# Opening products of two projection pairs moved into the end of the scan stage, and the block sums of the input loaded whole on GpSimd's queue

## The chip, the cores and the metric

The kernel runs on one core of one Trainium2 chip. The metric is the device time of one execution in microseconds (us), the median over several runs; lower is better. The engines of the core are PE (TensorE, matrix products), DVE (VectorE), ACT (ScalarE), POOL (GpSimd) and SP (SyncE, which here only issues DMAs). Each takes its own instructions in order. A DMA can be issued from several engines' queues; this kernel issues nearly all from SP, and eight accumulating stores from POOL.

## The reference

One layer of an encoder on 1024 tokens and 16 learned meta tokens, in float32, with a model width of 1024:

```python
h = rmsnorm(h_res, norm1_w[l])
proj = h @ w_in[l]
(q, k, v, z, b_raw, a_raw, sc_b, sc_c, sc_x, gate_a, gate_b) = jnp.split(proj, SPLIT_POINTS, axis=-1)
o_dn = gated_deltanet_bidir(q, k, v, z, b_raw, a_raw, ...)
y_a = o_dn @ w_branch_dn[l]
y_b = (sc_b * depthwise_conv_centred(sc_c * sc_x, sc_conv_w[l])) @ w_branch_sc[l]
merged = jax.nn.sigmoid(gate_a) * y_a + jax.nn.sigmoid(gate_b) * y_b
h_res = h_res + merged @ w_out[l]
gu = rmsnorm(h_res, norm2_w[l]) @ w_gate_up[l]
h_res = h_res + (jax.nn.silu(gu[..., :D_FF]) * gu[..., D_FF:]) @ w_down[l]
```

The gated DeltaNet has eight heads with a forward and a backward scan over chunks of 64 tokens; its output is normalized per head and multiplied by silu(z). A final norm follows, and the meta tokens are dropped.

## The kernel before, in words

**Stage 1** runs the eight heads' scans. Between the small products of the scans PE works through a stream of dense projections (L345): units of 128 columns of `w_in`, first those that the heads need (q, k, v), then `fill_units` (the short convolution, some gates, and z of the first `ZH` heads). Each unit's weights, 128x1024, are loaded by `pick` on SP into one of a few rotating `raw` slots and split in quarters into a high and a low part by `split_part`: ACT casts half of the chunk (128x512), DVE subtracts, twice. Every float32 product is made of three matmuls (high by high, high by low, low by high). A planner with a time per engine decides during the build what comes next; the instructions then stand in a fixed order on each engine.

A head ends with `outputs()`, its norm (`norm()` in `g_scan`: L942, L945, a root on small tiles at L516 to L521, then eight scalings at L950), eight transposes on PE (L98) into two banks, two copies `vS` (L965) and two stores of o_d. z of the same heads is finished by L481 (ACT), L485 and L487 (DVE) and stored in z_d.

The block sums of the input's four quarters (for the scheme below) are made early in stage 1 and stored in DRAM, as four tiles `tx_d0` to `tx_d3`.

**The border and stage 2.** The remaining projections are made in pairs: two units `rg` and `ru` of `w_in` by all 1024 tokens, as a 2x2 block product with seven block products instead of eight. P1 and P2 are plain blocks of rg by blocks of the input; S1 to S4 take sums of weight blocks (S4 by a plain input block), TT takes the plain last block of ru; T1 to T4 are the input's sums. Each of them is twelve matmuls of 128x512 (`product`, L1552). The first two pairs are z of the last heads ("z pairs", n = 0 and 1), then come the gates (n = 2, 3, ...). The engines' order at the border is written out by hand in `SECTION`, one name a step, the pair's number behind it: `h`, `l` split rg whole (ACT L1599, DVE L179, 128x1024); `uh`, `ul` split ru's last block (128x512, L1608); `b1` to `b4` are the weight sums on DVE (128x512 each, in place in rg and ru); `sah`, `sal`, `sbh`, `sbl` split those sums (L1616, 128x1024 each); `T1h` and `T1l`, and so on, split the input's sums (ACT L1573, DVE L179, 128x2048 each); `P1`, `P2`, `S1` to `S4`, `TT` are the products on PE; `c` and `a` take results out of the banks (L1629 on ACT, L1518 on DVE); the rest finishes outputs.

The tiles that these steps share are eight large homes (`b0` to `b3`, `mA`, `mB` and others): a step that writes a home waits until its last reader is through. In the kernel before, the sums are loaded at the border by 16 DMAs of 256 KB on SP (L1576), behind the last head's stores and ahead of the second pair's weights (L1593). The first pair's weights are loaded, and rg of them split, in stage 1.

Of the kernel before, what the change touches and what calls it, by code (L numbers as in the profile page):

```python
# [8 lines left out]
F32 = mybir.dt.float32  # L9
# [7 lines left out]
P = 128  # L17
D = 1024
# [30 lines left out]
def encoder_layer(ctx: ExitStack, tc: tile.TileContext, x, meta, norm1_w, w_in, w_ba,  # L49
# [442 lines left out]

    def cs(c):
# [302 lines left out]
    def g_scan(h, st_):  # L796
# [162 lines left out]
        for c4 in range(2):  # L959
            oT = vS[:, 4 * c4:4 * c4 + 4]  # L960
            pt = newbank()
            for c in range(4):
                transpose(pt[:, c], oacc[4 * c4 + c])
            yield pe(430)
            nc.scalar.copy(oT, pt)  # L965
            A(512)
            nc.sync.dma_start(o_d[h][:, c4 * 512:(c4 + 1) * 512].rearrange("p (c t) -> p c t", c=4), oT)
# [22 lines left out]
    def pick():  # L990
# [46 lines left out]
    def g_input_sums():  # L1037
# [17 lines left out]
        for k in range(4):  # L1055
            for x in range(2):
# [7 lines left out]
                for i in range(2):  # L1064
                    nc.sync.dma_start(part_of(tx_d[k][:, i], x), r[:, i])
                yield T["pe"] + LAND
# [489 lines left out]
    def moving_steps():  # L1556
# [3 lines left out]
        for i in range(2):  # L1560
            for j in range(2):
                mov[f"B{i + 1}{j + 1}"] = hx[0][:, 4 * i:4 * i + 4, c[j]], [hx[1][4 * i + k][:, c[j]] for k in range(4)]
        for g, n in (("b0", "T1"), ("b1", "T2"), ("mA", "T3")):
            t = big(g, [P, 2, 4, 512])
            mov[n] = t[:, 0], t[:, 1]
        x, y = (big(g, [P, 2, 4, 512], F32) for g in ("b2", "b3"))
        raws_ = {"T2": x[:, 0], "T1": x[:, 1], "T3": y[:, 0], "T4": y[:, 1]}

        def high(n, t):
            if n == "T4":  # L1570
                m = big("b2", [P, 2, 4, 512])
                mov[n] = m[:, 0], m[:, 1]
            nc.scalar.copy(mov[n][0], t)  # L1573
        for n, (r, c) in (("T2", (1, right)), ("T1", (0, left)), ("T3", (0, right)), ("T4", (1, left))):
            for k in range(4):
                nc.sync.dma_start(raws_[n][:, k], tx_d[k][:, r, c])  # L1576
# [3 lines left out]
    raw_slots.extend((tp, f"raw{i}") for i in range(2))  # L1580
    left, right = slice(0, 512), slice(512, 1024)
# [6 lines left out]
    def pair_steps(n, j, z=False):  # L1588

        A_, a = {}, {}  # L1590
        rg, ru = (rawtile([P, KT, P]) for _ in range(2))
        for r, off in zip((rg, ru), (OZ, OZ + P) if z else (OGA, OGB)):
            nc.sync.dma_start(r, w_in[unit(off + j * P)])  # L1593
        g0, g1, u0, u1 = rg[:, 0:4], rg[:, 4:8], ru[:, 0:4], ru[:, 4:8]
# [6 lines left out]
        def corner():  # L1601
            if n == 0:
                u = big("w2", [P, 2, 4, P])
                u_hl[0] = u[:, 0], u[:, 1]
            elif n == 1:
                u_hl[1] = [tp.tile([P, 4, P], F32R, tag="t2", name=uid("u_hl"), bufs=2) for _ in range(2)]
            A_["A22"] = u_hl[n % 2]
            nc.scalar.copy(u_hl[n % 2][0], u1)  # L1608
# [9 lines left out]
        def out_tile(k):  # L1618
            if k not in a:
                a[k] = s4()  # L1620
            return a[k]
# [57 lines left out]
    def last_pair(n, j):  # L1679
# [29 lines left out]
    SECTION = """  # L1709
        P1_0 uh_0 ul_0 b1_0 b2_0 P2_0 b3_0 h_1 b4_0 c1_0 l_1 sah_0 P1_1 sbh_0 sal_0 T2h sbl_0 a1_0 P2_1 T2l T1h  # L1710
        S2_0 T1l T3h uh_1 T3l S1_0 c2_0 T4h ul_1 S3_0 b1_1 c3_0 c1_1 b2_1 h_2 a1_1 h1_0 S4_0 l_2 h1_1 T4l P1_2 b3_1
        sbh_1 a3_0 b4_1 h3_0 P2_2 s1_0 sah_1 sbl_1 c1_2 sal_1 TT_0 a2_0 s1_1 h2_0 a1_2 s2_0 S2_1 uh_2 h4_0 ul_2 h1_2
        b1_2 b2_2 S1_1 c2_1 b3_2 sbh_2 b4_2 s3_0 sah_2 S3_1 sbl_2 c3_1 sal_2 S4_1 a3_1 s4_0 h3_1 s3_1 TT_1 a2_1 h2_1
        s2_1 S2_2 h4_1 s4_1 S1_2 c2_2 h_3 S3_2 l_3 c3_2 S4_2 a3_2 h3_2 TT_2 a2_2 h2_2 h4_2
    """
    first = [pair_steps(0, ZH, True)[0]]
    moving_steps()
    first.append(pair_steps(1, ZH + 2, True)[0])
# [56 lines left out]
    def head_load(h):  # L1775

        if not og:
            og.extend(big(f"b{2 + i}", [P, 4, SEQ], F32) for i in range(2))
        if h < ZH:
# [26 lines left out]
    def next_part():  # L1806
# [592 lines left out]
```

## Time and profile before

| | |
|---|---|
| median of 3 runs | 1971.52 us (1971.27 to 1975.44) |
| the profiled execution's own time | 1974.82 us |
| its span | 1972.8 us, mean granted clock 0.992 |
| PE busy | 1939.6 us, 98% of the span |
| DVE, ACT, POOL busy | 1481.7, 880.6, 116.3 us |
| stage 1's last dense matmul (L345) starts | 924.40 us |
| third pair's first product starts | 968.69 us |

The profile comes from the one execution of 1974.82 us. In its timeline a row has the start, the duration, the engine, the line, the operation with output and inputs, the count, and in brackets the engine's idle time ahead with what ended it. In the table of waits a row has the engine and line that waited, what released it, then us in all, how often, and the longest. L12 is line 12 of the kernel before; behind the change the lines are up to some 30 higher.

### The profile page before, as it was taken

Reading aid. Unit: us, or ns where it says so; the run is one execution under the profiler, and the core shown is the slowest. Engines: PE = TensorE matmul, PEld = TensorE weight load, DVE = VectorE, ACT = ScalarE, POOL = GpSimd, SP = SyncE. Lnnn points to the kernel's source line nnn. Section 1 sums busy time; section 2 is a strip of 40 time slices with the busy share of each in tenths; the row PEclk is TensorE's granted clock in tenths of the full one; section 3 lists DMA queues with packets and bytes.
Section 4 is the critical chain, followed back from the end, with each engine's and each line's share of the span. In section 5 each row is a group of like instructions: output and inputs, shape, how many; then the busy total and the mean of one; then the engine's idle time right before and its main releaser. Section 6 shows DMA issues by size and latency. Waiting matters only on the chain.

```text
span 1972.8 us, 32276 instructions
## 1 busy us (share of the span) xinstructions
PE 1939.6 (98%) x11872; PEld 1702.2 (86%) x11872; DVE 1481.7 (75%) x3158; ACT 880.6 (45%) x2026; POOL 116.3 (6%) x418
## 2 busy tenths in 40 slices
PE   9999999999999999999799999999999999999998
PEld 8998999999999999887688878788888888888886
DVE  7888688898989888867666688669676766746575
ACT  6462354636464646343444544235333333325344
POOL 2012201010101010200000000000000000000000
PEclk9999999999999999999899999999999999999999
DMA  4266322223232223376457955233366654577654
GB/s 145 67 173 153 92 87 81 98 81 97 81 108 60 76 60 98 114 260 226 156 190 271 355 205 183 95 100 115 108 232 246 245 182 160 175 280 240 195 175 163
DMA packets 155299, 307.13 MB, mean 156 GB/s; under 512 B 47932, under 2 KB 57589, under 8 KB 151685
## 3 DMA queue, kind: packets, MB, share of 16 engines
q1 hardware_dynamic: 153397, 299.83, 45.2%
q0 software_dynamic: 1152, 4.19, 1.3%
q8 instruction: 93, 1.52, 0.3%
q10 hardware_dynamic: 592, 1.05, 0.1%
q14 instruction: 65, 0.53, 0.1%
HBM read 211.60 MB, written 93.41 MB: 155 GB/s over the span
## 4 chain that ended last, share of the span: by engine, by line
PE 85%; DMA 6%; DVE 6%; issue 1%; ACT 1%; SPq 0%; DVEq 0%; ACTq 0%
PE pm L345 31%; PE pd L1552 13%; PE pe L1552 7%; PE pm L1552 4%; PE pe L612 1%; PE pd L914 1%; PE pd L893 1%; PE pd L875 1%; PE pd L878 1%; PE pe L2306 1%; PE pe L2308 1%; PE pe L2307 1%; PE pd L910 1%; PE pd L98 1%; PE pd L2306 1%
## 5 line engine op out<-in xcount | busy, mean ns | idle before, releaser
L345 PE MATMUL pm<-al,wh 128*128 128x320 f32 (+4 forms) x1248 | 426.5, 347 | 0.0
L345 PE MATMUL pm<-hTh,wh 128*128 128x320 f32 (+4 forms) x1248 | 425.5, 346 | 0.5 <-ACT hTh L1188 0.5
L345 PE MATMUL pm<-hTh,wl 128*128 128x320 f32 (+4 forms) x1248 | 424.3, 345 | 0.0
L345 PEld LDWEIGHTS pm<-hTh,wh 128*128 128x128 f32 x1248 | 233.7, 188 | 11.4 <-ACT hTh L1188 1.3
L345 PEld LDWEIGHTS pm<-hTh,wl 128*128 128x128 f32 x1248 | 233.9, 188 | 10.0
L345 PEld LDWEIGHTS pm<-al,wh 128*128 128x128 f32 x1248 | 233.9, 188 | 9.9
L102 DVE TENSOR_TENSOR al<-raw,ring_h 128x1024 fp32r<-128x1024 f32 x73 | 88.6, 1222 | 65.1 <-ACT ring_h L101 64.5
L101 ACT CAST ring_h<-raw 128x1024 fp32r<-128x1024 f32 x73 | 76.7, 1053 | 107.5 <-PE pd L2308 38.7
L367 DVE SCALAR_TENSOR_TENSOR kq<-ra,wc,kq 128x520 f32<-128x520 f32 x128 | 96.6, 754 | 3.6 <-ACT kq L397 2.1
L900 ACT ACTIVATE w<-pd,small 128x128 f32<-128x128 f32 x128 | 39.9, 363 | 126.7 <-PE pd L893 126.4
L1007 DVE TENSOR_TENSOR wl<-raw,wh 128x512 fp32r<-128x512 f32 x112 | 75.6, 686 | 18.7 <-ACT wh L1010 18.3
L505 DVE TENSOR_TENSOR tm<-fP,fN 128x135 f32<-128x135 f32 (+23 forms) x248 | 72.3, 292 | 7.3 <-DMA fN<-nd 2.0
L509 DVE TENSOR_TENSOR fP<-fP,tm 128x135 f32<-128x135 f32 (+23 forms) x248 | 71.9, 290 | 5.2
L1010 ACT CAST wh<-raw 128x512 fp32r<-128x512 f32 x112 | 66.3, 626 | 3.7 <-issue 3.6
L865 ACT ACTIVATE jk<-NP 128x128 f32<-128x128 f32 x64 | 19.9, 311 | 90.5 <-DVE NP L861 89.4
L2246 ACT ACTIVATE b<-b 128x512 f32<-128x512 f32 x20 | 12.6, 632 | 105.2 <-DVE b L1518 105.2
L1518 DVE TENSOR_TENSOR b<-pd,b 128x512 f32<-128x512 f32 x21 | 14.5, 689 | 51.9 <-PE pd L1552 51.8
L1552 PE MATMUL pd<-b_hl,wh 128*128 128x512 f32 x168 | 51.9, 390 | 0.0
L102 DVE TENSOR_TENSOR al<-raw,parts_h 128x1024 fp32r<-128x1024 f32 x28 | 33.5, 1218 | 24.3 <-ACT parts_h L101 24.3
L367 DVE SCALAR_TENSOR_TENSOR vT<-ra,wc,vT 128x520 f32<-128x520 f32 x64 | 48.3, 755 | 3.4 <-ACT vT L397 2.3
L555 ACT ACTIVATE PQ<-PQ,negG 128x128 f32<-128x128 f32 x128 | 43.3, 395 | 16.8 <-DVE PQ L550 16.7
L701 POOL TENSOR_TENSOR tm<-mP,mN 1x15 f32<-1x15 f32 (+7 forms) x120 | 37.2, 310 | 205.9 <-DMA mN<-ndm 197.6
(678 smaller groups left out, 4853.3 us busy)
## 6 DMA issues: line engine op xcount, KB each, us to landing
raw<-in_w_in_dram SPq DMA_DIRECT2D x72, 512.0 KB
raw<-in_w_gate_up_dram SPq DMA_DIRECT2D x44, 512.0 KB
sums<-in_w_down_dram SPq DMA_DIRECT2D x22, 512.0 KB
t_d<-sums SPq DMA_DIRECT2D x11, 1024.0 KB
raw<-s_d SPq DMA_DIRECT2D x44, 256.0 KB
raw<-t_d SPq DMA_DIRECT2D x44, 256.0 KB
act_d<-b SPq DMA_DIRECT2D x43, 256.0 KB
raw<-act_d SPq DMA_DIRECT2D x33, 256.0 KB
```

The costliest lines, as they stand in the source:

```text
L101: nc.scalar.copy(hi, src)
L102: nc.vector.tensor_tensor(out=lo, in0=src, in1=hi.bitcast(F32), op=ALU.subtract)
L345: mm(po[:, :n], ww[:, k], f(k)[:, t0:t0 + n], start=i == 0, stop=i == 3 * KT - 1)
L367: nc.vector.scalar_tensor_tensor(out=acc, in0=raw[:, h0 + t:h0 + t + hn], scalar=wc[:, t, col:col + 1], in1=acc, op0=ALU.mult, op1=ALU.add)
L505: nc.vector.tensor_tensor(out=tv, in0=fP[:, 0:r, j:j + 1].broadcast_to([P, r, n]), in1=fN[:, j:j + 1, j + 1:32].broadcast_to([P, r, n]), o ...
L509: nc.vector.tensor_tensor(out=fP[:, 0:r, j + 1:32], in0=fP[:, 0:r, j + 1:32], in1=tv, op=ALU.subtract)
L555: nc.scalar.activation(PQ[:, c, d], PQ[:, c, d], AF.Exp, bias=negG2[:, c, hd:hd + 1])
L900: nc.scalar.activation(w[d], b2[:, 2 + d], AF.Copy, scale=ce[:, c, d:d + 1])
L1007: nc.vector.tensor_tensor(out=u[1][1][:, k], in0=u[2][:, k], in1=u[1][0][:, k].bitcast(F32), op=ALU.subtract)
L1010: nc.scalar.copy(u[1][0][:, k], u[2][:, k])
L1552: mm(po, x[:, k], at(y, k), start=i == 0 and not add_to, stop=i == 11, skip_group_check=add_to)
L2306: mm(bank[t], h_[:, c], h_[:, hi], start=first, stop=False)
```

## The change

1. Two more units are appended to the dense stream, `u_open` for rg of both z pairs. They are held until the last head's `outputs()` are through (`tail["on"]`) and then make P1 and P2 of both pairs (48 matmuls). Their weights are loaded by `pick` and split by `split_part` in stage 1.
2. `tx_d` becomes one tile in DRAM; each of the four sums is loaded whole, 1 MB in rows of 2 KB, by one DMA on GpSimd's queue. ru of both z pairs is loaded behind them on the same queue.
3. The last head's transposes go to the two `pe` banks instead of those of its scan.
4. `SECTION` has a new order, and the homes of T1 to T4, of the pair sums and of some later tiles are renamed to fit.

The diff, cut to its core:

```diff
-    tx_d = [dr.tile([P, 2, D], F32, name=f"tx_d{i}") for i in range(4)]
+    tx_d = dr.tile([4, P, 2, D], F32, name="tx_d")
...
+    tail, opened = {"on": False}, []
+
+    def u_open(w):
+
+        while not tail["on"]:
+            T["pe"] += 100
+            yield
+        a = {"g": w, "bank": pss(), "p2": psm()}
+        opened[[x.get("g") for x in opened].index(None)].update(a)
+        c = slice(C0 + META, C0 + META + 512)
+        for po, k0 in ((a["bank"], 0), (a["p2"], 4)):
+            for i in range(12):
+                k, m = k0 + i // 3, i % 3
+                mm(po, w[m == 2][:, k], hx[0][:, k, c] if m != 1 else hx[1][k][:, c], start=i == 0, stop=i == 11)
+                pe(227)
+                yield
...
         outputs()
+        tail["on"] = h == H - 1
...
-            pt = newbank()
+            pt = psd().rearrange("p (a n) -> p a n", a=4) if h == H - 1 else newbank()
...
+    fill_units += [(OZ + h * P, u_open, None, None) for h in (ZH, ZH + 2)]
...
         nc.sync.dma_start(raw, w_in[unit(u[0])])
+        if u[1] is u_open:
+            opened.append({"raw": raw})
...
-        for g, n in (("b0", "T1"), ("b1", "T2"), ("mA", "T3")):
-            t = big(g, [P, 2, 4, 512])
-            mov[n] = t[:, 0], t[:, 1]
-        x, y = (big(g, [P, 2, 4, 512], F32) for g in ("b2", "b3"))
+        t = big("b0", [P, 2, 4, 512])
+        mov["T1"] = t[:, 0], t[:, 1]
+        x, y = (big(g, [P, 2, 4, 512], F32) for g in ("b1", "mA"))
+        t = big("b2", [P, 2, 4, 512])
+        mov["T2"] = t[:, 0], t[:, 1]
...
-        for n, (r, c) in (("T2", (1, right)), ("T1", (0, left)), ("T3", (0, right)), ("T4", (1, left))):
-            for k in range(4):
-                nc.sync.dma_start(raws_[n][:, k], tx_d[k][:, r, c])
+        for n, (r, c) in (("T3", (0, right)), ("T4", (1, left)), ("T2", (1, right)), ("T1", (0, left))):
+            nc.gpsimd.dma_start(raws_[n], tx_d[:, :, r, c].rearrange("k p c -> p k c"))
...
-        rg, ru = (rawtile([P, KT, P]) for _ in range(2))
-        for r, off in zip((rg, ru), (OZ, OZ + P) if z else (OGA, OGB)):
-            nc.sync.dma_start(r, w_in[unit(off + j * P)])
+        if z:
+            rg, ru = opened[n]["raw"], rawtile([P, KT, P])
+            nc.gpsimd.dma_start(ru, w_in[unit(OZ + P + j * P)])
+            a.update({k: opened[n][k] for k in ("g", "bank", "p2")})
...
     SECTION = """
-        P1_0 uh_0 ul_0 b1_0 b2_0 P2_0 b3_0 h_1 b4_0 c1_0 l_1 sah_0 P1_1 sbh_0 sal_0 T2h sbl_0 a1_0 P2_1 T2l T1h
-        S2_0 T1l T3h uh_1 T3l S1_0 c2_0 T4h ul_1 S3_0 b1_1 c3_0 c1_1 b2_1 h_2 a1_1 h1_0 S4_0 l_2 h1_1 T4l P1_2 b3_1
...
+        uh_0 ul_0 b1_0 T2h b2_0 b3_0 b4_0 c1_0 T2l sah_0 sbh_0 sal_0 S2_0 T1h sbl_0 T3h T1l S1_0 c2_0 a1_0 uh_1 T3l
+        T4h h_2 S3_0 c3_0 T4l ul_1 l_2 S4_0 a3_0 b1_1 c1_1 h1_0 b2_1 P1_2 b3_1 sbh_1 b4_1 h3_0 sah_1 a1_1 P2_2 sbl_1 c1_2
...
```

**PE at the end of stage 1.** Before, behind the last dense matmul (NP is the head's output, ident the identity of a transpose; pd, pe and pm are banks):

```order
L345 MATMUL pm_12188<-hTh,wl_11936 128x512
L98 MATMUL pd_12282<-ident,NP_10513 128x128 x4
L98 MATMUL pd_12289<-ident,NP_10513 128x128
L1552 MATMUL pd_12346<-hTh,wh_12342 128x512
L98 MATMUL pd_12289<-ident,NP_10513 128x128 x3
L1552 MATMUL pd_12346<-al_148,wh_12342 128x512
```

With the change, first the start of the 24 matmuls that follow the last dense one, then, of the second pair's, the place of the transposes and the end:

```order
L345 MATMUL pm_12191<-hTh,wl_11933 128x512
L506 MATMUL pd_12273<-hTh,wh_12102 128x512
...
L506 MATMUL pd_12320<-al_145,wh_12271 128x512
L98 MATMUL pe_12334<-ident,NP_10510 128x128 x4
L506 MATMUL pd_12320<-hTh,wl_12272 128x512
L98 MATMUL pe_12342<-ident,NP_10510 128x128 x4
L506 MATMUL pm_12321<-hTh,wh_12271 128x512
...
L506 MATMUL pm_12321<-hTh,wl_12272 128x512
L1573 MATMUL pd_12273<-b_2080_12373,b_2081_12378 128x512 x12
```

The transposes stood ahead of nearly all opening products; now 35 of the 48 stand ahead of them, and the product behind the last (L1573) is S2 of the first pair.

**The loads.** Before, on SP, behind the last stores:

```order
L489 DMA z_d_114<-rb_12265 128x512
L967 DMA o_d_126<-vS_11705 128x512 x2
L1576 DMA b_2072_12312<-tx_d_91 128x512
L1576 DMA b_2072_12312<-tx_d_92 128x512
...
L1593 DMA raw_12330<-in_w_in_dram 128x1024
L1593 DMA raw_12331<-in_w_in_dram 128x1024
```

Now they are the last DMAs on POOL, behind two memsets of the last head:

```order
L745 MEMSET XT_11423 32x8x32
L1597 DMA mA_12372<-tx_d 128x4x512 x2
L1597 DMA b_2078_12371<-tx_d 128x4x512 x2
L1614 DMA raw_12379<-in_w_in_dram 128x1024
L1614 DMA raw_12381<-in_w_in_dram 128x1024
```

Nothing on POOL's queue waits for the last head's stores of o_d any more; ru of the first pair (the first L1614) stands behind all four sums.

**DVE at the border.** With the change, from the last small operation of the root on:

```order
L538 SCALAR_TENSOR_TENSOR small_10219<-small_10219 128x9
L968 TENSOR_SCALAR NP_10510<-NP_10510,small_10219 128x128 x7
L1028 TENSOR_TENSOR wl_12272<-raw_12104,wh_12271 128x512 x2
L968 TENSOR_SCALAR NP_10510<-NP_10510,small_10219 128x128
L179 TENSOR_TENSOR w_2088_12387<-raw_12379,w_2088_12387 128x512
L1539 TENSOR_TENSOR raw_12379<-raw_12379 128x512
L179 TENSOR_TENSOR raw_12379<-raw_11934,raw_12379 128x512
L179 TENSOR_TENSOR raw_11934<-raw_12379,raw_11934 128x512
L179 TENSOR_TENSOR raw_11934<-raw_11934 128x512
L179 TENSOR_TENSOR b_2080_12373<-b_2078_12371,b_2080_12373 128x2048
L179 TENSOR_TENSOR b_2081_12378<-raw_11934,b_2081_12378 128x1024
```

Before, the eight scalings (there L950) stood in one row and the weight sums followed; the low half of the second pair's rg (there one subtraction of 128x1024) came behind the sums. Now its two halves stand ahead of the last scaling, and T2's low part (128x2048) ahead of the pair sum's (the last row). In the orders after the first pairs no instruction has moved on any engine.

More of the change, by code (lines that the diff above doesn't have):

```diff
@@ L1064, in g_input_sums @@
                 for i in range(2):
-                    nc.sync.dma_start(part_of(tx_d[k][:, i], x), r[:, i])
+                    nc.sync.dma_start(part_of(tx_d[k, :, i], x), r[:, i])
                 yield T["pe"] + LAND
@@ L1590, in pair_steps @@
         A_, a = {}, {}
-        rg, ru = (rawtile([P, KT, P]) for _ in range(2))
-        for r, off in zip((rg, ru), (OZ, OZ + P) if z else (OGA, OGB)):
-            nc.sync.dma_start(r, w_in[unit(off + j * P)])
+        if z:
+            rg, ru = opened[n]["raw"], rawtile([P, KT, P])
+            nc.gpsimd.dma_start(ru, w_in[unit(OZ + P + j * P)])
+            a.update({k: opened[n][k] for k in ("g", "bank", "p2")})
+            gh, gl = a["g"]
+            A_["A11"], A_["A12"] = (gh[:, 0:4], gl[:, 0:4]), (gh[:, 4:8], gl[:, 4:8])
+        else:
+            rg, ru = (rawtile([P, KT, P]) for _ in range(2))
+            for r, off in ((rg, OGA), (ru, OGB)):
+                nc.sync.dma_start(r, w_in[unit(off + j * P)])
         g0, g1, u0, u1 = rg[:, 0:4], rg[:, 4:8], ru[:, 0:4], ru[:, 4:8]
@@ L1601, in corner @@
         def corner():
[L1602 to L1606, printed above, removed]
             A_["A22"] = u_hl[n % 2]
@@ L1619, in out_tile @@
             if k not in a:
-                a[k] = s4()
+                a[k] = first_out if n == 0 and k == "o1" else s4()
             return a[k]
@@ L1709, in encoder_layer @@
     SECTION = """
-        P1_0 uh_0 ul_0 b1_0 b2_0 P2_0 b3_0 h_1 b4_0 c1_0 l_1 sah_0 P1_1 sbh_0 sal_0 T2h sbl_0 a1_0 P2_1 T2l T1h
-        S2_0 T1l T3h uh_1 T3l S1_0 c2_0 T4h ul_1 S3_0 b1_1 c3_0 c1_1 b2_1 h_2 a1_1 h1_0 S4_0 l_2 h1_1 T4l P1_2 b3_1
-        sbh_1 a3_0 b4_1 h3_0 P2_2 s1_0 sah_1 sbl_1 c1_2 sal_1 TT_0 a2_0 s1_1 h2_0 a1_2 s2_0 S2_1 uh_2 h4_0 ul_2 h1_2
-        b1_2 b2_2 S1_1 c2_1 b3_2 sbh_2 b4_2 s3_0 sah_2 S3_1 sbl_2 c3_1 sal_2 S4_1 a3_1 s4_0 h3_1 s3_1 TT_1 a2_1 h2_1
+        uh_0 ul_0 b1_0 T2h b2_0 b3_0 b4_0 c1_0 T2l sah_0 sbh_0 sal_0 S2_0 T1h sbl_0 T3h T1l S1_0 c2_0 a1_0 uh_1 T3l
+        T4h h_2 S3_0 c3_0 T4l ul_1 l_2 S4_0 a3_0 b1_1 c1_1 h1_0 b2_1 P1_2 b3_1 sbh_1 b4_1 h3_0 sah_1 a1_1 P2_2 sbl_1 c1_2
+        sal_1 s1_0 TT_0 a2_0 h1_1 h2_0 a1_2 S2_1 s2_0 h4_0 s1_1 uh_2 ul_2 S1_1 c2_1 h1_2 b1_2 b2_2 b3_2 sbh_2 b4_2 s3_0 sah_2
+        S3_1 sbl_2 c3_1 sal_2 S4_1 a3_1 s4_0 h3_1 s3_1 TT_1 a2_1 h2_1
         s2_1 S2_2 h4_1 s4_1 S1_2 c2_2 h_3 S3_2 l_3 c3_2 S4_2 a3_2 h3_2 TT_2 a2_2 h2_2 h4_2
     """
-    first = [pair_steps(0, ZH, True)[0]]
     moving_steps()
-    first.append(pair_steps(1, ZH + 2, True)[0])
+    first_sums = big("b3", [P, 2, 2, KT, P])
+    first = [pair_steps(n, ZH + 2 * n, True)[0] for n in range(2)]
+    u_hl[1] = [tp.tile([P, 4, P], F32R, tag="t2", name=uid("u_hl"), bufs=2) for _ in range(2)]
+    first_out = s4()
+    t3_hl = big("mB", [P, 2, 4, 512])
+    mov["T3"] = t3_hl[:, 0], t3_hl[:, 1]
+    u = big("w2", [P, 2, 4, P])
+    u_hl[0] = u[:, 0], u[:, 1]
+    rot["i"] = 2
     first.extend(pair_steps(n, GH + n - 2)[0] for n in (2, 3))
@@ L1777, in head_load @@
         if not og:
-            og.extend(big(f"b{2 + i}", [P, 4, SEQ], F32) for i in range(2))
+            og.extend(big(g, [P, 4, SEQ], F32) for g in ("b3", "b1"))
         if h < ZH:
@@ L1811, in next_part @@
         if i in (0, 1, 3, 4):
-            tag = ("b1", "b0")[i // 3]
+            tag = ("b2", "b0")[i // 3]
             if tag not in early:
@@ L1866, in out_split @@
         if j % 4 == 0:
-            for w, tags in ((woh, ("b2", "b0")), (wol, ("b1", "b3"))):
+            for w, tags in ((woh, ("b3", "b0")), (wol, ("b2", "b1"))):
                 t = big(tags[j // 4], [P, 4, D])
```

10 lines of the change are left out of this document (4 added, 6 removed).

## The prediction

> **What bounds the kernel now.** I read the waits of the tensor engine (PE) first, since the page has it busy 98% of the span.
>
> ```profile
> PE 1939.6 (98%) x11872; PEld 1702.2 (86%) x11872; DVE 1481.7 (75%) x3158; ACT 880.6 (45%) x2026; POOL 116.3 (6%) x418
> PE pd L1552 <- ACT wh L1599: 11.5, 1, 11.5
> PE pd L98 <- DVE NP L950: 3.6, 1, 3.6
> PE pd L1980 <- DVE wl L102: 2.1, 1, 2.1
> ```
>
> The two longest waits, 15.1 us together, stand at the border that the change rewrites; every other one is 2.1 us or less. Next, PE's timeline there.
>
> ```profile
> 924.40 0.39 PE L345 MATMUL pm<-hTh,wl 128*128 128x512 f32 x1
> 928.43 1.33 PE L98 MATMUL pd<-ident,NP 128*128 128x128 f32 x5 [3.65 <-DVE NP L950]
> 932.76 0.63 PE L1552 MATMUL pd<-hTh,wh 128*128 128x512 f32 x1
> 933.19 0.63 PE L1552 MATMUL pd<-al,wh 128*128 128x512 f32 x1
> 937.49 0.39 PE L1552 MATMUL pe<-hTh,wl 128*128 128x512 f32 x1
> 949.37 0.79 PE L1552 MATMUL pd<-hTh,wh 128*128 128x512 f32 x1 [11.50 <-ACT wh L1599]
> 957.81 2.88 PE L1552 MATMUL pd<-b,mB 128*128 128x512 f32 x12
> 960.53 2.88 PE L1552 MATMUL pe<-b,mB 128*128 128x512 f32 x12
> 968.69 0.39 PE L1552 MATMUL pd<-hTh,wh 128*128 128x512 f32 x1
> ```
>
> Stage 1's last matmul ends at 924.8. A product of twelve takes 2.72 us (960.53 less 957.81), so 0.227 a matmul; after each wait the pitch is 0.43 (932.76 to 933.19). From the row that the third pair's first product opens (968.7) nothing stops PE, so I date the end of the border there. The windows show the clock and the transfers:
>
> ```profile
> 918.66:924.78 6.12, 6.12 (x33) 4.90 (x31) 3.48 (x13) 2.68 (x12) 0.00 (x0) 1.00 0.11 43
> 928.43:937.88 9.45, 9.44 (x32) 7.40 (x32) 4.78 (x12) 1.69 (x3) 0.00 (x0) 0.68 0.63 199
> 937.88:949.37 11.49, 0.00 (x0) 0.00 (x0) 0.02 (x1) 1.09 (x2) 0.00 (x0) 0.65 0.94 354
> 949.37:957.97 8.60, 8.55 (x25) 6.38 (x26) 8.40 (x6) 8.26 (x7) 0.00 (x0) 0.67 0.37 124
> ```
>
> After the two times are busy PE, PEld, DVE, ACT and POOL, then the granted clock, the DMA share and GB/s. In the long wait DVE and ACT do nothing and the DMA engines are 94% busy: PE waits for bytes, with a clock of 0.65 to 0.68 around it. The chain of waits says which bytes.
>
> ```profile
> 918.18 0.45 PE pd L878 x4
> 928.09 0.30 DVE NP L950
> 930.87 0.59 ACT vS L965
> 931.98 4.46 DMA b<-tx_d
> 936.51 5.75 DMA b<-tx_d
> 942.28 5.97 DMA raw<-in_w_in_dram
> 948.28 1.05 ACT wh L1599
> ```
>
> The last head's norm (L950), its transposes, the copy (L965) and the store stand ahead of the loads on SP's queue; then 16 loads of tx_d and the second pair's weights go out. From the first issue (931.98) to the landing of those weights (948.25) pass 16.3 us for 4.19 + 0.52 MB.
>
> **The change, step by step.** The sum is made against the profiled execution, 1974.82 us (span 1972.8). That is 3.3 above the median 1971.52, whose neighbour is 1971.27, so only the difference is carried over to the median.
>
> *PE's opening products.* Their 48 matmuls are only moved: P1_0 and P2_0 (24) now follow the last L345 at once, 924.8 to 930.2 at 0.227. This fills the 3.65 wait. The weights they need were loaded and split before: the first pair's L1599 and L179 stood in stage 1 already, and the second pair's (two 128x512 casts, two subtractions) are new there. That price falls on DVE's order, below. P1_1's third matmul takes the low half wl_1, which DVE now makes between the seventh and eighth L950.
>
> ```profile
> 924.32 0.17 DVE L945 SCALAR_TENSOR_TENSOR small<-small 128x9 f32<-128x9 f32 x1 [0.69 <-ACT jk L865]
> 928.09 1.66 DVE L950 TENSOR_SCALAR NP<-NP,small 128x128 f32<-128x128 f32 x8
> 932.00 0.69 DVE L179 TENSOR_TENSOR w<-raw,w 128x512 fp32r<-128x512 f32 x1 [2.25 <-ACT w L1608]
> 932.73 0.69 DVE L1518 TENSOR_TENSOR raw<-raw 128x512 f32<-128x512 f32 x1
> 950.78 2.36 DVE L179 TENSOR_TENSOR mB<-raw,mB 128x1024 fp32r<-128x1024 f32 x2 [0.20 <-ACT mB L1616]
> 953.66 4.48 DVE L179 TENSOR_TENSOR b<-b,b 128x2048 fp32r<-128x2048 f32 x2
> ```
>
> Before, L945 to the end of L950 took 924.32 to 929.75, 5.4 us, with one 128x512 pair (L485, L487) inside. Now one half of wl_0 (0.65) goes ahead and the seventh L950 ends at 931.3; the two halves of wl_1 (some 0.6 each, a little under the 0.69 row, since neither reads the other) follow. PE has 2 matmuls of P1_1 to do from 930.2, then waits 1.3 us, runs nine more (to 934.0), four transposes, one matmul, four transposes, and P2_1's twelve to 937.9. That is where before's opening stood after *one* pair.
>
> *Which wait ends last then.* S2_0 needs the pair sum that ACT casts as sah_0 and DVE splits as sal_0. ACT has both vS copies ahead of uh_0, and each waits for its four transposes:
>
> ```profile
> 929.59 0.59 ACT L965 COPY vS<-pd 128x512 f32<-128x512 f32 x1 [4.16 <-PE pd L98]
> 931.35 0.62 ACT L1608 CAST w<-raw 128x512 fp32r<-128x512 f32 x1
> 949.70 1.99 ACT L1616 CAST mB<-raw 128x1024 fp32r<-128x1024 f32 x2
> 951.60 3.70 ACT L1573 CAST b<-b 128x2048 fp32r<-128x2048 f32 x2
> ```
>
> Copies 934.7 and 935.4, so uh_0 starts at 936.0 and ul_0 at 936.7. Then DVE is the chain: ul_0 (0.68), four block sums (b1 to b4, 0.72 each: 932.00 to 932.73) to 940.2, T2l (2.2, half of 4.48) to 942.4, sal_0 (1.1 to 1.2, half of 2.36) to 943.5; beside it ACT makes T2h (1.85, half of 3.70), c1_0 (0.5) and sah_0 (0.95) by 941.2. S2_0 opens at 941.3, after 3.4 us without work, has its second matmul at 942.4 and its third at 943.6, and ends at 947.5 with the half pitch for the first 5.5 us, as after the 3.65 wait. DVE keeps ahead from there: sbl_0 944.7, T1l 946.9 (S1_0 wants it at 947.5), a1_0, T3l 949.7 (S3_0's second matmul: 950.4), T4l 952.8, ul_1, l_2 954.6 (P1_2 wants it at 955.8). Products of 2.72 from 947.5: S1_0, S3_0, S4_0, and P1_2 at 955.6. **Gain: 968.8 less 955.6, 13.2 us.** If the pitch stays at 0.227, S2_0 ends 0.7 sooner: 13.9. If S2_0 followed P2_1 at once, 20: no more can come from here.
>
> *The loads on GpSimd's queue (POOL).* T3, T4, T2, T1 (1 MB each), then ru_0 and ru_1 (0.52 each). The first waits for the last L878 product (row above: ends 918.6) and for the last store of sd_d, issued at 911.87, 6.8 us before; behind it on POOL stand only its own kind. The DMA engines are 11% busy then. Before's trace has no plain load on this queue. Nearest rows:
>
> ```profile
> 911.87 0.40 SPq L1094 DMA_DIRECT2D sd_d<-kq  x1
> 931.98 9.96 SPq L1576 DMA_DIRECT2D b<-tx_d  x16
> q0 software_dynamic: 1152, 4.19, 1.3%
> 133.94 0.88 POOL L1043 DMA_DIRECT2D hx_d<-al  x1
> 135.15 0.86 POOL L1043 DMA_DIRECT2D hx_d<-al  x1 [0.33 <-DMA hx_d<-hTh]
> DMA to landing us min/median/max: 5.3/5.7/8.2
> ```
>
> The same 4.72 MB took 16.3 us on SP's queue, so ru_0 lands at 918.7 + 16.3 = 935.0, 0.9 before ACT is free for it. The other end is the accumulating stores, the only users of q0: 1.3% of 1972.8 is 25.6 us of all engines for 4.19 MB, 164 GB/s; 4.72 MB at that take 28.8 and, with 2.5 us of fixed landing (5.7 less 3.2 of its own bytes), ru_0 is there at 950.0. These rows read and add their target too, which a plain load does not, so I take the first. Between them: 0.87 us of POOL for 144 packets (1152 by 8) is 3.2 for a T load's 528, if it grows with packets; five issues then end near 932.3 and ru_0 lands near 937. Whatever is later than 935.9 costs one to one; from 949.1 on the gain is gone.
>
> [...]
>
> *The rest.* POOL issues in 918 to 935, where its busy time is 0.00. rg_2 on SP waits for sal_0 (943.5); with the row of 5.97 for weights it is there at 949.5, before h_2 (950.6). ru_2 is loaded only after sal_1 (961.2): landed 967.2, its chain of the same six DVE steps ends near 974.3, S2_2 wants it at 977.4: hidden with 3 us over. The orders behind the pairs are equal on every engine.
>
> **The rivals.** (a) *Loads late by some microseconds*: POOL's issue grows with packets, or transfers of stage 1 share the engines; ru_0 at 938 to 945, gain 4 to 11. For it: the unknown price; against: 0.11 share and 13 us of lead. (b) *The accumulating rate holds*: ru_0 at 950.0, gain 13.2 less 14.1: 1972.4, no change. (c) *The queue takes one transfer at a time*, the slower end: each T load waits for the one ahead. A megabyte then takes 5.7 + 1.3 (0.52 MB more at some 400 GB/s), four of them and ru_0's 5.7 make 33.7, ru_0 at 952.4, 3.3 us **slower**: 1974.8; with 8.2 for 5.7, 15.8 slower. Against it: two issues 1.2 us apart, where a strict queue would make the second's landing 5.7 + 5.7 - 1.2 = 10.2, and none is above 8.2. It decides from 7.6 us per T load on. [...] (e) *DVE's chain is longer than my sum*, by a hop at each of eight steps: 1 to 2 us less. (f) The order has the 24 matmuls right behind the last L345, so that the change doesn't do what it says is left out.
>
> **How the numbers follow.** Forecast with (d) and (e), gain 11 to 15: 0.70; (a) 0.14; (b) 0.07; (c) 0.05; above 15: 0.04. The likeliest gives 1971.5 - 13.2 = 1958.3. Eight in ten: up from 1955.0 (gain 16.5, half of what lies between 13.2 and 20) to 1966.0 (gain 5.5, most of (a)). A measurement of this kernel can tell 0.2%, 3.9 us. Faster by more: 0.70 + 0.04 + nearly all of (a), 0.87; same: (b) and a rest of (a), 0.07; slower: (c) with its far end and the mishap of (b), 0.06.
>
> **What would show it.** PE's waits: no row of 11.5; one of about 1.3 at the third matmul of P1_1, released by DVE; S2_0 opening at 941 to 942, released by ACT or DVE and not by a transfer. POOL's first T load at 918.7, ru_0 landed before 936. P1_2 near 955.6, TT_0, S2_1 and S2_2 without a wait, and all later stages 13 us earlier. Wrong: uh_0 released by the DMA of ru_0 (a, b, c), T loads landing over 7 us apart (c), POOL's issue much over 0.9 us (a, d), a wait before S2_2 for ru_2.

## The result, and the profile after

The changed kernel takes 1962.85 us (1960.38 to 1963.21) against 1971.97 us for the kernel before: a ratio of 0.9948, 95% interval 0.9930 to 0.9965, so 7 to 14 us faster. Measured again on another chip, it took 1962.37 us against 1971.67: 0.9946 (0.9934 to 0.9959). The forecast was 1958.3, with a range of 1955.0 to 1966.0. The gain is real and inside the range, and some 4 us smaller than forecast.

The profiled execution took 1963.04 us, with a span of 1961.3. Its table of PE's waits, then PE's timeline at the border:

```profile
PE pd L1573 <- ACT b L1639: 5.4, 1, 5.4
PE pe L98 <- DVE xr L1195: 2.1, 1, 2.1
PE pd L2008 <- DVE wl L102: 2.1, 1, 2.1
...
PE pd L506 <- DVE wl L1028: 0.9, 1, 0.9
```

```profile
924.87 0.39 PE L345 MATMUL pm<-hTh,wl 128*128 128x512 f32 x1
925.09 0.39 PE L506 MATMUL pd<-hTh,wh 128*128 128x512 f32 x1
...
932.02 0.50 PE L506 MATMUL pd<-hTh,wl 128*128 128x512 f32 x1 [0.88 <-DVE wl L1028]
...
937.86 0.39 PE L506 MATMUL pm<-hTh,wl 128*128 128x512 f32 x1
943.67 0.79 PE L1573 MATMUL pd<-b,b 128*128 128x512 f32 x1 [5.43 <-ACT b L1639]
944.80 0.80 PE L1573 MATMUL pd<-b,b 128*128 128x512 f32 x1 [0.33 <-DVE b L179]
945.93 4.63 PE L1573 MATMUL pd<-b,b 128*128 128x512 f32 x10 [0.34 <-DVE b L179]
950.37 3.41 PE L1573 MATMUL pe<-b,b 128*128 128x512 f32 x12
953.61 2.88 PE L1573 MATMUL pd<-mB,b 128*128 128x512 f32 x12
...
959.05 0.39 PE L1573 MATMUL pd<-hTh,wh 128*128 128x512 f32 x1
```

The waits of 3.6 and 11.5 us are gone. What stands in their place is 0.9 us at the second pair's low half, where the prediction had 1.3, and one of 5.4 us ahead of S2 of the first pair, where it had 3.4. The opening products follow the last L345 without a gap and end at 938.1.

Stage 1 does not end at the same time in every execution, so I measure the border by one distance: from the start of the last L345 row to the start of the third pair's first product. Before it was 968.69 - 924.40 = 44.3 us, now it is 959.05 - 924.87 = 34.2. That is 10.1 us, of the 13.2 that the prediction's sum gave.

The reason stands in three views of the changed kernel: POOL's timeline, the one row of ACT's on which the chain hangs, and the sum of all transfers from 925 to 938.

```profile
922.43 1.63 POOL L1597 DMA_DIRECT2D mA<-tx_d  x2 [104.06 <-DMA rb<-o_d]
924.04 0.76 POOL L1597 DMA_DIRECT2D b<-tx_d  x1
928.52 0.75 POOL L1597 DMA_DIRECT2D b<-tx_d  x1 [3.72 <-issue]
929.26 1.09 POOL L1614 DMA_DIRECT2D raw<-in_w_in_dram  x2
```

```profile
938.29 0.62 ACT L1631 CAST w<-raw 128x512 fp32r<-128x512 f32 x1 [2.17 <-DMA raw<-in_w_in_dram]
```

```profile
DMA packets 1421, 5.17 MB, mean 397 GB/s; under 512 B 96, under 2 KB 96, under 8 KB 1421
```

The first load of a sum went out at 922.4 and not at 918.7. From there to the landing of ru_0 (938.27) pass 15.8 us, against the 16.3 that the prediction took from SP's queue, at 397 GB/s while the bytes run. The transfer was sized rightly; its start was not. ACT, free at 936.1 as the prediction says, then waits 2.17 us for ru_0.

### The profile page after: what moved, and what is told of

Same layout as the page of the kernel before. It is cut to its first block, busy times and chain, and to the rows that moved or that the text cites. A ratio compares the mean times of both kernels' runs of the same rounds, so it can differ in the third digit from the quotient of the medians.

```text
span 1961.3 us, 32258 instructions
## 1 busy us (share of the span) xinstructions
PE 1934.9 (99%) x11872; PEld 1697.2 (87%) x11872; DVE 1482.2 (76%) x3160; ACT 881.5 (45%) x2028; POOL 118.1 (6%) x424
## 3 DMA queue, kind: packets, MB, share of 16 engines
q10 hardware_dynamic: 592, 1.05, 0.1%
## 4 chain that ended last, share of the span: by engine, by line
PE 85%; DVE 6%; DMA 5%; issue 2%; ACT 1%; SPq 0%; POOL 0%; DVEq 0%; POOLq 0%; ACTq 0%
PE pm L345 30%; PE pd L1573 14%; PE pe L1573 7%; PE pm L1573 4%; PE pe L629 1%; PE pd L931 1%; PE pe L2335 1%; PE pe L2336 1%; PE pe L2334 1%; PE pd L892 1%; PE pd L910 1%; PE pd L895 1%; PE pd L927 1%; PE pd L2335 1%; PE pd L2336 1%
## 5 line engine op out<-in xcount | busy, mean ns | idle before, releaser
L345 PE MATMUL pm<-al,wh 128*128 128x320 f32 (+4 forms) x1248 | 426.4, 347 | 0.0
L345 PE MATMUL pm<-hTh,wh 128*128 128x320 f32 (+4 forms) x1248 | 425.4, 346 | 0.4 <-ACT hTh L1209 0.2
L345 PE MATMUL pm<-hTh,wl 128*128 128x320 f32 (+4 forms) x1248 | 424.4, 345 | 0.1
L345 PEld LDWEIGHTS pm<-hTh,wh 128*128 128x128 f32 x1248 | 233.7, 188 | 11.0 <-ACT hTh L1209 0.9
L345 PEld LDWEIGHTS pm<-hTh,wl 128*128 128x128 f32 x1248 | 233.8, 188 | 10.4 <-POOL wl L1224 0.3
L345 PEld LDWEIGHTS pm<-al,wh 128*128 128x128 f32 x1248 | 233.9, 188 | 9.9
L882 ACT ACTIVATE jk<-NP 128x128 f32<-128x128 f32 x64 | 19.9, 311 | 90.1 <-DVE NP L878 89.1
L1573 PE MATMUL pd<-b_hl,wh 128*128 128x512 f32 x168 | 51.9, 390 | 0.0
```

The costliest lines, as they stand in the source:

```text
L345: mm(po[:, :n], ww[:, k], f(k)[:, t0:t0 + n], start=i == 0, stop=i == 3 * KT - 1)
L1573: mm(po, x[:, k], at(y, k), start=i == 0 and not add_to, stop=i == 11, skip_group_check=add_to)
```

## The experiments

In the table, "distance" is the one defined above, from each kernel's profile, and "ratio" is to runs of the kernel before on the same chip. Times in us.

| kernel | distance | time | before | ratio, 95% interval |
|---|---|---|---|---|
| before | 44.3 | | | |
| changed | 34.2 | 1962.85 | 1971.97 | 0.9948 (0.9930 to 0.9965) |
| early_home | 35.4 | 1964.60 | 1973.71 | 0.9954 (0.9940 to 0.9969) |
| loads_on_SP | 46.8 | 1974.16 | 1973.71 | 1.0007 (0.9997 to 1.0016) |
| loads_only | 37.1 | 1965.57 | 1973.71 | 0.9956 (0.9939 to 0.9972) |
| kept_busy | 33.2 | 1959.62 | 1973.71 | 0.9932 (0.9917 to 0.9947) |
| ru_first | 31.8 | 1958.22 | 1971.67 | 0.9925 (0.9911 to 0.9939) |
| late_copies | 28.4 | 1958.31 | 1971.67 | 0.9924 (0.9911 to 0.9936) |
| changed_again | 32.6 | 1962.37 | 1971.67 | 0.9946 (0.9934 to 0.9959) |
| other_home | 26.3 | 1956.27 | 1972.53 | 0.9909 (0.9895 to 0.9922) |

### early_home: when the first load can go

```diff
+        for g in ['mA', 'b1', 'b0', 'b2']:
+            big(g, [P, 2, 4, 512])
         t = big("b0", [P, 2, 4, 512])
```

The order in which the homes are named first sets their place in memory, and with it which tiles of stage 1 lay there.

> Edit: the homes b0 and mA change places in memory, so that the first two loads of block sums (T3, T4) no longer wait for the last store of sd_d, but for the last head's L873 (ends about 918.2 in the changed kernel's profile). Theory A, the late start: ru_0 landed at 938.3 because the first load went out at 922.4 and not at 918.7; here the first load goes out at 918 to 919, ru_0 lands at 934 to 935, ACT no longer waits for it, S2_0 opens near 941.3, the third pair's first product starts near 956.5 instead of 959.1, and the time falls by 2.5 to 3 us. Rival B, GpSimd's queue itself sets the landing (the 3.7 us for which it held the fourth load): ru_0 still lands at 937 or later and the time falls by less than 1 us.

The timeline of this kernel, one row of POOL's and one of PE's (start, duration, engine, line, operation, and in brackets the wait ahead with what ended it):

```profile
924.12 1.63 POOL L1599 DMA_DIRECT2D mA<-tx_d  x2 [105.59 <-ACT jk L882]
945.77 0.80 PE L1573 MATMUL pd<-b,b 128*128 128x512 f32 x1 [7.76 <-ACT b L1641]
```

The edit went the wrong way. I had taken the pair of L873 at 917.6 for the head's last, and its last one runs at 922.8 here. The trace puts the wait down to L882, which follows that pair and ends at 924.07, so the first load went out 1.7 us *later* than in the changed kernel. It still answers the question, with the sign turned round: start 1.7 later, ru_0 taken at 940.40 and not 938.29 (2.1 later), S2_0 opened at 945.77 and not 943.67 (2.1 later). The landing follows the start, as theory A has it. The changed kernel's second profile (changed_again, below) agrees: start 1.6 earlier (920.79), ru_0 taken 1.6 earlier (936.67). The hold on the fourth load is there in both (3.82 and 3.72 us) and explains no difference between them.

### loads_on_SP: the opening products without GpSimd's queue

```diff
-            nc.gpsimd.dma_start(raws_[n], tx_d[:, :, r, c].rearrange("k p c -> p k c"))
+            nc.sync.dma_start(raws_[n], tx_d[:, :, r, c].rearrange("k p c -> p k c"))
...
-            nc.gpsimd.dma_start(ru, w_in[unit(OZ + P + j * P)])
+            nc.sync.dma_start(ru, w_in[unit(OZ + P + j * P)])
```

> Edit: the changed kernel with its six loads on SP's queue, where they stand behind the last head's two stores of o_d. Theory: the opening products alone bring nothing, since S2_0 waits for ru_0: the loads go out at 936, ru_0 lands 16 us later at 952, S2_0 opens at 957 to 958, the third pair starts at 972 to 973, and the time is 2 to 4 us above the kernel before (about 1975). Rival: the opening products in stage 1 are worth their matmul time by themselves: the third pair starts at 962 or earlier, and the time stays within 3 us of the changed kernel's.

SP's queue in this kernel's timeline, and then ACT and PE in the same:

```profile
935.16 1.00 SPq L985 DMA_DIRECT2D o_d<-vS  x2
936.27 1.02 SPq L1597 DMA_DIRECT2D mA<-tx_d  x2
937.34 1.43 SPq L1597 DMA_DIRECT2D b<-tx_d  x2
938.89 2.64 SPq L1614 DMA_DIRECT2D raw<-in_w_in_dram  x2
```

```profile
951.05 0.62 ACT L1631 CAST w<-raw 128x512 fp32r<-128x512 f32 x1 [15.23 <-DMA raw<-in_w_in_dram]
956.42 0.80 PE L1573 MATMUL pd<-b,b 128*128 128x512 f32 x1 [18.48 <-ACT b L1639]
```

Behind the last head's stores the loads go out at 936.3, ru_0 is there at 951.0, and one wait of 18.5 us has taken the place of both old ones. The distance is 2.5 us longer than before, and the time is not told from before (1.0007). The theory's place nearly holds (third pair at 971.3, not 972 to 973); its 2 to 4 us above the kernel before are not shown. Moving 48 matmuls (10.9 us) into stage 1 is worth nothing as long as the next operand comes when it came before.

### loads_only: GpSimd's queue without the opening products

```diff
-            for k in range(4):
-                nc.sync.dma_start(raws_[n][:, k], tx_d[k][:, r, c])
+            nc.gpsimd.dma_start(raws_[n], tx_d[:, :, r, c].rearrange("k p c -> p k c"))
```

(on the kernel before, with `tx_d` as one tile).

> Edit: the kernel before, with nothing changed but that the four sums are loaded whole on GpSimd's queue (no opening products, old order and homes). Theory: the wait of 11.5 us was for the second pair's weights behind 4.2 MB on SP's queue; now they go out near 932 and share the engines with the sums: they land at 938 to 941, the second pair's opening products start at 939 to 942 instead of 949.4, the third pair at 959 to 962, and this alone brings 7 to 10 us. Rival: both parts are needed, since the weights now share the engines with the sums from the first byte: they land after 945 and it brings less than 4 us.

This kernel's table of PE's waits (number of waits and longest behind the sum):

```profile
PE pd L1552 <- ACT wh L1598: 4.1, 1, 4.1
PE pd L98 <- DVE NP L950: 3.7, 1, 3.7
```

The wait of 11.5 us falls to 4.1: the second pair's weights go out at 932.7 and land at 941.6, though they share the engines with the sums. The distance falls by 7.2 us and the time by 0.44% (0.28 to 0.61). So of the 10.1 us that the whole change takes out of the border, some 7 come with the place of the loads alone. The rest comes only when the opening products, with the new order and homes, are added to it; by themselves they brought nothing (loads_on_SP). In the time that rest is not shown: the intervals of loads_only and of the changed kernel overlap.

### kept_busy: the clock

```diff
+    def busy():
+        po = psd()
+        for _ in range(20):
+            mm(po, opened[1]["g"][0][:, 0], mov["B11"][0][:, 0], start=True, stop=True)
...
-        ... sbh_0 sal_0 S2_0 T1h ...
+        ... sbh_0 sal_0 busy S2_0 T1h ...
```

> Edit: the changed kernel with 20 idle matmuls of 128x512 (their result is read by nobody) in the 5.4 us ahead of S2_0. Theory: the wait also costs clock; with PE busy S2_0's last ten matmuls run at a pitch of 0.227 and not 0.43, S2_0 and S1_0 take 2.5 us less between them, of which DVE's splits of T1, T3 and T4 then give back about half: third pair at 957.5 instead of 959.1, time 1 to 2 us lower. Rival: the slow pitch comes from operands that arrive late, or from the throttle as such: pitch and time stay as in the changed kernel.

The windows of the changed kernel; the columns are as in the prediction, and the granted clock is the third number from the end.

```profile
940.00:942.00 2.00, 0.00 (x0) 0.00 (x0) 1.90 (x4) 1.19 (x2) 0.00 (x0) 0.78 0.03 11
946.00:948.00 2.00, 2.00 (x5) 1.61 (x6) 2.00 (x2) 2.00 (x2) 0.00 (x0) 0.50 0.55 137
951.00:952.00 1.00, 1.00 (x5) 0.76 (x5) 1.00 (x1) 1.00 (x3) 0.00 (x0) 0.82 0.04 16
```

The same view of kept_busy:

```profile
942.00:944.00 2.00, 1.09 (x6) 0.59 (x4) 1.97 (x3) 1.15 (x2) 0.00 (x0) 1.00 0.00 0
944.00:946.00 2.00, 0.93 (x2) 0.31 (x2) 2.00 (x2) 2.00 (x2) 0.00 (x0) 1.00 0.00 0
946.00:947.00 1.00, 0.80 (x3) 0.66 (x4) 1.00 (x2) 1.00 (x2) 0.00 (x0) 0.81 0.00 0
950.00:951.00 1.00, 1.00 (x6) 0.82 (x5) 1.00 (x2) 0.61 (x2) 0.00 (x0) 0.98 0.77 315
```

With the idle matmuls the clock stays at 1.00 from 942 to 946, where the changed kernel shows 0.50, so here the throttle does follow PE's work. But behind them S2_0's first three matmuls still stood up to 1.1 us apart, and the clock fell at 946.6 instead, just as the ten ran. The distance is 33.2, between the changed kernel's two profiles (34.2 and 32.6), so the gain that I expected is not shown by it; the time's interval overlaps too. So the outcome is the rival's, a slow pitch and a time that is not told apart. Of the rival's two causes, late operands are out: the clock fell within the ten, and where it stayed at 1.00 (other_home, below) the ten took 2.56 us and not 4.15, though they too had just waited for DVE. The throttle is what is left.

### ru_first: what lands first

```diff
-        for n, (r, c) in (("T3", (0, right)), ("T4", (1, left)), ("T2", (1, right)), ("T1", (0, left))):
+        def fetch(n, r, c):
             nc.gpsimd.dma_start(raws_[n], tx_d[:, :, r, c].rearrange("k p c -> p k c"))
+
+        late_loads.extend((lambda: fetch("T2", 1, right), lambda: fetch("T1", 0, left), lambda: fetch("T3", 0, right),
+                           lambda: fetch("T4", 1, left)))
...
-    first = [pair_steps(n, ZH + 2 * n, True)[0] for n in range(2)]
+    first = [pair_steps(0, ZH, True)[0]]
+    for f in late_loads:
+        f()
+    first.append(pair_steps(1, ZH + 2, True)[0])
```

The four loads of sums, collected in `late_loads` in the order T2, T1, T3, T4, now stand behind ru_0.

> Edit: the order of the loads on GpSimd's queue alone: ru of the first pair first, then T2, T1, T3, T4, then ru of the second pair. Theory A (S2_0 is late because ru_0 lands behind 4 MB that start late): the queue's first load still goes out at about 923, now for L931, but ru_0 lands at 927 to 929, ACT takes it as soon as both vS copies are done (936.1), S2_0 opens near 941.4 instead of 943.7 and has its third matmul near 943.7, the third pair starts at 956 to 957.5 (959.1 in the changed kernel), and the time falls by 1.5 to 3 us. Rival: T2's high part then takes the place of ru_0 (its load lands later than 937), and the third pair starts no earlier than 958.5.

The timeline of this kernel on POOL, ACT and PE:

```profile
922.27 0.62 POOL L1618 DMA_DIRECT2D raw<-in_w_in_dram  x1 [104.85 <-issue]
933.49 1.26 ACT L983 COPY vS<-pe 128x512 f32<-128x512 f32 x2 [7.93 <-PE pe L98]
934.65 0.62 ACT L1635 CAST w<-raw 128x512 fp32r<-128x512 f32 x1
940.03 0.50 PE L1573 MATMUL pd<-b,b 128*128 128x512 f32 x1 [3.15 <-ACT b L1643]
```

ACT takes ru_0 right behind the copies, without a wait, and PE's wait ahead of S2_0 is 3.15 us: what the prediction had (3.4). The distance is 31.8, where its sum gives 31.2 (955.6 less 924.40). Beside each other on one chip this kernel took 1958.22 and the changed one 1962.37, with intervals that overlap at their ends (up to 0.9939, and from 0.9934). So the time that was forecast for the change, 1958.3, is that of this order of loads. At the border the gain over the changed kernel's two profiles is 0.8 to 2.4 us; why the medians lie 4 apart is not shown.

### late_copies and other_home: the next in line

```diff
             yield pe(430)
+            if h == H - 1:
+                turned_last.append(pt)
+                continue
             nc.scalar.copy(oT, pt)
...
-        uh_0 ul_0 b1_0 T2h b2_0 b3_0 b4_0 c1_0 T2l ...
+        uh_0 ul_0 b1_0 T2h b2_0 v1 v2 b3_0 b4_0 c1_0 T2l ...
```

This is ru_first with the copies v1 and v2 (and their stores, on GpSimd's queue) moved behind T2's high part.

> Edit: ru_first, and the last head's two vS copies are moved on ACT behind uh_0 and T2's high part (their stores go through GpSimd's queue). Theory: after the loads, the next in line is ACT, which holds uh_0 behind copies that wait for the transposes: here uh_0 runs near 929 to 931, ul_0 follows the last scaling (932.8), the block sums end at 936.4, sal_0 at 939 to 940, S2_0 opens at 938 to 939 with a third matmul near 940, PE stays idle for less than 3 us, the clock stays at 1.00, and the third pair starts at 951 to 953: 6 to 8 us below the changed kernel. Rival: T2's home waits for z_d's last stores or the scalings, T2h and with it the copies and sah_0 come no earlier than in ru_first: third pair at 955 or later.

ACT's row of T2's high part in this kernel's timeline:

```profile
934.91 1.91 ACT L1598 CAST b<-b 128x2048 fp32r<-128x2048 f32 x1 [7.42 <-DMA z_d<-rb]
```

uh_0 now runs at 926.9 and the block sums end at 935.7, but T2's high part waited for z_d's last store, whose tile lay in T2's home, and took the chain over. That is the rival's mechanism, but not its outcome: the third pair starts at 952.7, inside the theory's 951 to 953, and the distance is 28.4 against 31.8. What failed of the theory is the clock, which fell at 940.7 for 3.4 us, and the time, which is 4 and not 6 to 8 us below the changed kernel. Then the homes change places (`for g in ['b0', 'b1', 'mA', 'b3', 'b2']: big(g, [P, 2, 4, 512])` ahead of the first use):

> Edit: late_copies, and the homes b2 and b3 change places in memory, so that T2's high part no longer waits for z_d's last store and the last scaling (in late_copies it ran at 934.9, released by that store), but only for its load and an earlier store; the pair sum's home takes that wait and is wanted later. Theory: T2h runs at 930 to 933, T2l right behind the block sums (935.7), sal_0 by 939, S2_0's first matmul follows P2_1 within 0.5 us and its third within 1.7 us, the clock stays at 1.00, and from the last L345 to the third pair pass 26 to 27.5 us (28.4 in late_copies, 44.3 before); time 1956 to 1957.5, a step below late_copies that a comparison of this size may not resolve. Rival: T2's load itself lands after 934, since the stores of z_d and the sums share the engines, and nothing changes.

ACT and PE in this kernel's timeline:

```profile
931.99 1.92 ACT L1600 CAST b<-b 128x2048 fp32r<-128x2048 f32 x1 [4.88 <-DMA b<-tx_d]
938.61 2.56 PE L1576 MATMUL pd<-b,b 128*128 128x512 f32 x10 [0.63 <-DVE b L179]
941.95 2.79 PE L1576 MATMUL pe<-b,b 128*128 128x512 f32 x11 [0.55 <-DVE b L179]
```

T2's high part waits for its own load alone, S2_0's ten matmuls run in 2.56 us instead of 4.63, and the distance is 26.3, below the changed kernel's two profiles (34.2 and 32.6) by 7.9 and 6.3 us. 1956.27 us, ratio 0.9909, is the best of all kernels here, with an interval that lies wholly below the changed kernel's in both of its comparisons. Against ru_first and late_copies the intervals overlap.

### changed_again

> The changed kernel once more beside the two before it, for a comparison on the same chip: 9 to 12 us below the kernel before, third pair at 959 to 960.

The difference is 9.3 us; the third pair starts at 956.1, since stage 1 ended 1.35 us earlier in this execution. The distance differs by 1.6 us from that of the first profile of the same code, and the clock explains most of it: S2_0's ten matmuls took 3.82 us here and 4.63 there, S1_0 2.88 and 3.41. Third pair at 959 to 960 was thus missed, the time was not.

## Why the prediction was right or wrong, point by point

- **What bounds the kernel** (bytes for the second pair behind 4.2 MB on SP's queue): right. loads_only takes the sums off that queue and nothing else, and the wait falls from 11.5 to 4.1 us; loads_on_SP leaves them there and gains nothing.
- **The opening products**: right. They start at 925.1, wait 0.88 us for wl_1 where the sum had 1.3, and end at 938.1 where it had 937.9.
- **ACT free for uh_0 at 936.0, and DVE's chain behind it**: right. The copies end at 936.1; from ul_0 to the end of sal_0 the sum had 936.7 to 943.5, 6.8 us, and the trace has 938.94 to 945.9, 7.0 us.
- **The loads' rate on GpSimd's queue**: right. "The same 4.72 MB took 16.3 us on SP's queue" was taken for it, and it was 15.8. Rivals (b) and (c) are out.
- **The loads' start**: this is the step that failed. "ru_0 lands at 918.7 + 16.3 = 935.0" took the last L878 product for the condition that ends last and gave the store of sd_d as good as done, "issued at 911.87, 6.8 us before". In the changed kernel that store is issued at 913.15, behind 0.5 MB of weights that the change itself loads there (912.14), and the first load went out at 922.43. The prediction counted those weights on DVE and ACT, and not on SP's queue ahead of the store. The windows of the kernel before, and then of the changed one, show what they did (the last two numbers are the DMA share and GB/s):

```profile
917.00:918.00 1.00, 1.00 (x8) 0.86 (x7) 0.73 (x3) 0.60 (x1) 0.00 (x0) 1.00 0.17 53
918.00:919.00 1.00, 1.00 (x11) 1.00 (x10) 0.61 (x2) 0.00 (x0) 0.00 (x0) 1.00 0.03 10
```

```profile
918.00:919.00 1.00, 1.00 (x10) 0.96 (x9) 0.52 (x3) 0.14 (x1) 0.00 (x0) 1.00 0.97 391
921.00:922.00 1.00, 1.00 (x6) 0.82 (x5) 0.44 (x1) 1.00 (x5) 0.00 (x0) 1.00 0.04 16
```

  Before, the engines were all but quiet from 918, so taking the store as done fits that kernel; with the change they were full until 919 and moved a last trickle until 922. No run moved the weights away to prove it. The lateness cost 2.3 us one to one at S2_0's third matmul (945.93, not 943.6). The trace puts the wait down to a load of o_d issued 0.7 us behind the store on the same queue; the program's own condition is the store. The two were not told apart by a run.
- **The clock behind the wait**: the term was mis-sized. The sum had 3.9 us for S2_0's last ten matmuls and 2.72 for S1_0; the chain of waits of the changed kernel, below, has 4.63 and 3.21 (start, length, engine and tile). That is 1.2 us more, and with the 2.3 it makes up the 3.5 us by which the third pair (959.05) is later than the sum's 955.6.

```profile
945.93 4.63 PE pd L1573 x10
950.57 3.21 PE pe L1573 x12
953.77 2.72 PE pd L1573 x12
```

- **The rivals**: the outcome is the upper edge of (a), "ru_0 at 938 to 945, gain 4 to 11", to which I gave 0.14, by a cause that (a) does not name (neither POOL's issue nor shared engines behind the start, but the start itself). The gain of 11 to 15, to which I gave 0.70, did not come, and the sign named for being wrong did: uh_0 was released by the DMA of ru_0. The range held the time because it took in most of (a). The forecast and the signs name a (d), POOL's issue drawn out; no run shows it: POOL's issues of a sum took 0.75 to 0.85 us each, from 923 to 924 with DVE busy all of that 1.00 us beside them, and the engines ran at 397 GB/s.
- **Two slips in the working**, on which the forecast does not hang: "It decides from 7.6 us per T load on" divides the 30.4 us from 918.7 to 949.1 by the four sums alone, and with ru_0's own 5.7 it is 6.2; and "a T load's 528" packets are 272 by the trace of the changed kernel (1376 on the queue, less two times 144 for the weights).
- **From the border to the median**: the prediction carried the border's gain over whole. The profiled pair differs by 11.5 us of span, 10.1 at the border; stage 1 ended 0.5 later, and all behind the third pair took 1.9 less. The order there is unchanged, and the distances from the third pair to the end lie between 1001 and 1005 us over all ten profiles, whatever the kernel. That part is no effect of the change.

## What to carry to other kernels

Work that is moved into an earlier stage is worth only what the next operand allows: first find what the product behind the moved ones waits for, and when that transfer can *start*, by what last lay in its destination and what the change itself puts ahead of that on its queue. On a queue that carries megabytes, order the loads by the time at which they are needed: here one small load moved ahead of four large ones (ru_first) brought the median from 1962.4 to 1958.2 us without a byte less, though the two intervals overlap at their ends.

## What the runs showed of the hardware that was not expected

**The half clock lasted 3.4 us or a multiple of it.** From the share of a window with a granted clock between 0.50 and 1.00 follows the moment at which it changed: in the changed kernel 0.78 in 940 to 942 puts the fall at 941.1, and 0.82 in 951 to 952 the return at 951.4. So the clock of 0.50 lasted 10.24 us there; worked out in the same way 13.68 us before (behind the wait of 11.5), 10.24 in early_home, 6.84 in loads_only, 3.42 in kept_busy: to within 0.03 three, four, three, two and one times 3.413, a third of the 10.24. In these five profiles the half clock was therefore not as long as the wait ahead of it but a number of whole steps: three behind a wait of 5.4 us (changed) as behind one of 7.8 (early_home). How many differs between executions of the same code: in the changed kernel's second profile the twelve of S1_0 run at the full pitch (2.71 us) from 947.97, 5.9 us behind the opening of S2_0, and in the first the clock came back only 7.7 us behind it. The prediction took "the half pitch for the first 5.5 us, as after the 3.65 wait"; the profile before has 6.84 us of it there, two steps (0.84 in 927 to 928 puts the fall at 927.7, 0.74 in 934 to 935 the return at 934.5).

The same wait of 2.10 us, much later in the program, shows it in two kernels with equal orders there. ru_first keeps its clock behind it, late_copies does not. PE's row in the timeline of ru_first, and a window behind it:

```profile
1224.55 0.50 PE L2015 MATMUL pd<-b,wl 128*128 128x512 f32 x1 [2.10 <-DVE wl L102]
```

```profile
1226.00:1228.00 2.00, 2.00 (x10) 1.63 (x9) 2.00 (x4) 0.00 (x0) 0.00 (x0) 1.00 0.30 119
```

The same two of late_copies:

```profile
1222.73 0.50 PE L2024 MATMUL pd<-b,wl 128*128 128x512 f32 x1 [2.10 <-DVE wl L102]
```

```profile
1224.20:1226.20 2.00, 2.00 (x6) 1.52 (x6) 2.00 (x5) 0.00 (x0) 0.00 (x0) 0.50 0.24 94
```

What differs is where the wait lies among the steps. In late_copies two falls lie whole steps apart (940.7 and 1224.0, 83 of 3.413), and before as well (941.3 and 1238.3, 87), so the steps can be counted on from the border. The wait of late_copies lies wholly in one step, 1220.6 to 1224.0. In ru_first the twelve of S1_0 took 3.15 us and not 2.72, which puts the return of the clock near 947.6 and the end of a step, 81 further on, near 1224.1; by this estimate the wait is cut into 1.7 and 0.4 us. Five profiles have windows around this wait: in the three that lose the clock behind it (before, late_copies, changed_again) at least 1.9 us of it lie in one step, in the two that keep it at most 1.7 (1.4 in the changed kernel, with 1.00 from 1228 to 1232).

One step at half clock costs PE up to 1.7 us, an estimate: half of a step. It may be one reason why late_copies, 3.4 us shorter at the border than ru_first, has the same median, and why single executions of one kernel differ by a few us; that it is the only one was not shown.

**GpSimd's queue held the fourth megabyte.** Three loads of 1 MB went out 0.8 us apart, and the fourth 3.7 us late (the row at 928.52 above), 0.4 us behind the landing of the first (5.7 us from its start); the two loads of weights then followed at once, with three megabytes still under way, so it is not a count of transfers. In ru_first, where a load of weights goes first, the fourth megabyte was held 6.1 us (it went out at 931.56). Counted by transfers that have not landed, it is no number of packets either: a sum has 272 and a load of weights 144 (1376 on the queue in all), so three sums and two weights (1104) went where four sums (1088) did not. What sets the hold stays open. It cost nothing here, since the engines were full (a share of 1.01 to 1.05 from 925 to 929). On SP's queue all six went out without such a hold, from 936.27 to 941.53 (loads_on_SP). An issue took 0.75 to 0.85 us for a megabyte of 272 packets and 0.55 for 144 packets: the bound "3.2 for a T load's 528, if it grows with packets" was far off.
